# Two transformer blocks on one core: side work placed by an estimate of the engines' times instead of by fixed steps

## The chip, the cores and the metric

The kernel runs on one core of one Trainium2 chip. The metric is the device time of one execution in microseconds (us), the median of several runs; lower is better. In the rows, PE is TensorE (matmuls; PEld is its loading of weights, which overlaps them), DVE is VectorE, ACT is ScalarE, POOL is GpSimd and SP is SyncE, which here only issues weight loads.

## What is computed

One call runs two transformer blocks over 256 tokens of width 2048, all in fp32. Cut to what matters:

```python
# first block
proj = rms_norm(x) @ w_in                      # attention q, k, v; hgrn q, f, i, g; two gates
y_attn = sliding_window_attention(rotary(q), rotary(k), v, sinks)
o = hgrn2_recurrence(hq, hf, hi, lb)           # a gated linear recurrence, 8 heads of 128
y_hgrn = rms_norm(o) * silu(hg)
merged = sigmoid(gate_a) * (y_attn @ w_ab) + sigmoid(gate_b) * (y_hgrn @ w_hb)
x = x + rms_norm(merged @ w_out)
x = x + rms_norm((silu(gate) * up) @ w_down)   # feed-forward
x = x + rms_norm((p @ w_pp) * sigmoid(rms_norm(x) @ w_pg))
# second block
proj = rmsnorm(x) @ w_in_2                     # sparse attention (indexer, top 64 keys) and fox attention
x = x + concat(dsa_mixer(...), fox_mixer(...)) @ w_o
x = x + conv_ffn(rmsnorm(x))                   # conv of width 3 over tokens between w_up and w_down
return rmsnorm(x, final_g)
```

## The kernel before

All weights are read once, in pieces of 256 rows by 512 columns. SP loads a piece into a staging tile `stg`; ACT rounds it to fp32r in a `ring` tile (L283); DVE subtracts to get the rest (L289); and PE multiplies in `Core.step` (L335) with three products each of high and low parts, for one of the two tiles t of 128 tokens. One such step is six matmuls of 128x512, and order prints it as one row with x6; the pieces and the steps on PE follow a list made before anything is emitted (`Core.plan`). A cast is written AHEAD_HI = 12.0 us ahead of the step that reads it, by the list's own time, and its DVE counterpart 11.0 us ahead.

Everything else is side work: norms, the transposes of activations (L350), softmax, the recurrence, the gates, the conv. Each piece of it is a Python generator. While `Core.run` writes the weight steps, it calls `Core.pump` once for each TICK = 1.4 us of the list's time, about once a step. A generator that says `yield N` is left alone for N pumps. What it writes when it goes on enters all engines' queues there, so N sets how many steps stand on PE between a side product and its reader, and also how many casts stand ahead of the reader on ACT. Engines run their queues in order. Where a generator asks for a PSUM bank (`get("sd")`), it waits until the bank has been given back in program order. Before the change N is a constant for each place: 3 in the recurrence `hgrn` between the decays and the products that read them, SWA_LEAD = 7 and Y_SOFT = 7 in the attention `swa`, FLIP_OUT = 5 and FLIP_IN = 10 around the two DMAs of a token transpose.

Three places matter below. In `hgrn` a half-step is: two matmuls L813 and L814, ACT's Exp L817, two products of its result, on POOL L820 and on DVE L821, then `yield 3`, then the small matmuls L827 that read both products. Two such chains w = 0, 1 run side by side, with 16 half-steps each. In `swa` the transposes L610 are evacuated by ACT (L612) and read by L626 and L627; later transposes L660 to L662 are evacuated by L663 and read by L670. In `conv` (and in the first feed-forward's `gate`) a projected tile, written by ACT at L1231, is transposed by DVE (L366), written to DRAM by POOL (L370), read back by POOL (L376), and then copied and scaled by ACT (L1560, L1565).

Of the kernel before, what the change touches and what calls it, by code (L numbers as in the profile page):

```python
# [18 lines left out]
P = 128  # L19
# [7 lines left out]
SWA_LEAD = 7  # L27
# [6 lines left out]
Y_SOFT = 7  # L34
# [3 lines left out]
B_LEAD = 1  # L38
LO_LAG = 2
FLIPS = 8  # L40
FLIP_OUT = 5
FLIP_IN = 10
# [5 lines left out]
N_COLS = 171 + 3 * 88  # L48

# [34 lines left out]
class Core:  # L84
    def __init__(self, ctx, tc, aps, out):
        self.tc, self.nc, self.i, self.out = tc, tc.nc, aps, out
        nc = self.nc
        self.mq = nc.gpsimd
# [40 lines left out]
    def take(self, cls, dt=F32):  # L129
        if cls in self.free_banks:  # L130
            self.free_banks[cls] -= 1
            self.serial += 1
            return self.psum.tile([P, 512], F32, tag=cls, bufs=4, name=f"{cls}_{self.serial}")
# [11 lines left out]
    def get(self, cls, n=1, dt=F32):  # L145
        while not self.can(cls, n):
            yield 1
        r = [self.take(cls, dt) for _ in range(n)]
        return r[0] if n == 1 else r

    def put(self, cls, n=1):
# [3 lines left out]
        else:  # L155
            self.free_banks[cls] += n
            assert self.free_banks[cls] <= 4, cls
# [10 lines left out]
    def col(self, n):  # L168
# [4 lines left out]
        return r  # L173

# [21 lines left out]
    def pump_until(self, cond, what):  # L196
        for _ in range(20000):
            if cond():
                return
            self.pump()  # L200
# [178 lines left out]
    def x_block(self, src, xt, j, t, goff):  # L379
# [5 lines left out]
        while xt.blk[j] is True:  # L385
            yield 1
        bank = yield from self.get("sd")
# [127 lines left out]
    def start(self):  # L515
        nc = self.nc
        sl = [slice(512 * j, 512 * j + 512) for j in range(4)]
        for j in range(4):
# [3 lines left out]
            yield 2  # L522
        for t in range(2):
# [20 lines left out]
    def head_kv(self, c):  # L544
# [3 lines left out]
        def done(t):  # L548
# [10 lines left out]
            yield 7  # L559
# [38 lines left out]
    def swa(self, q, rot):  # L598
# [20 lines left out]
        for pr in range(4):  # L619
            j = 4 * q + pr  # L620
            qt = qts[pr // 2][:, (pr % 2) * 256 : (pr % 2) * 256 + 256]
            l0, l1 = yield from self.get("s2", 2)
# [31 lines left out]
            yield Y_SOFT  # L654
            t0, t1 = yield from self.get("s2", 2)
            b0 = yield from self.get("sd")
            b1 = yield from self.get("sd")
# [9 lines left out]
            yield 3  # L667
# [23 lines left out]
    def head_hq(self, c, g):  # L691
# [3 lines left out]
        def done(t):  # L695
# [6 lines left out]
            yield 4  # L702
# [8 lines left out]
    def head_hf(self, c, g):  # L711
# [4 lines left out]
        def done(t):  # L716
            here.append(t)
            if len(here) == 1:
                return
            G = self.grp(g)  # L720
            yield from self.wait("lb")
            lb, om = yield from self.get("s2", 2)
            for a, r in enumerate((lb, om)):
                self.mq.dma_start(r, bass.AP(tensor=self.d_lb.tensor, offset=self.d_lb.offset + 1024 * a + 512 * g,
                                             ap=[[0, P], [1, 512]]))
# [12 lines left out]
            G["lf"] = yield from self.get("s8", dt=F32R)  # L738
            hi = G["lf"][:, 0:1024].rearrange("p (t n) -> p t n", t=2)
# [5 lines left out]
            yield 7  # L745
            while "qk" not in G:
                yield 1
            for u in range(2):
                bank = yield from self.get("sd")
# [44 lines left out]
    def hgrn(self, g, w):  # L794
# [4 lines left out]
        for hh in (w, w + 2):  # L799
# [5 lines left out]
            for t in range(2):  # L805
                kt, qt = k[:, t * P : (t + 1) * P], q[:, t * P : (t + 1) * P]
                pick = sc[:, t * P : (t + 1) * P]
                for half in range(2):
                    e = yield from self.get("sd")
# [12 lines left out]
                    yield 3  # L822
# [16 lines left out]
                    if half == 1 and t == 1:  # L839
                        x = yield from self.get("sd")  # L840
# [5 lines left out]
            yield 2  # L846
# [17 lines left out]
            yield 2  # L864
# [32 lines left out]
    def branch(self, c, ab, j, first):  # L897
# [13 lines left out]
        def done(t):  # L911
# [13 lines left out]
            yield 4  # L925
# [54 lines left out]
    def boundary(self, t):  # L980
# [14 lines left out]
        yield B_LEAD  # L995
# [29 lines left out]
    def ffn_up(self, c, i):  # L1025
# [3 lines left out]
        def done(t):  # L1029
# [7 lines left out]
            yield FLIP_OUT  # L1037
# [7 lines left out]
            yield FLIP_IN  # L1045
# [29 lines left out]
    def ple_p(self):  # L1075
# [3 lines left out]
        for t in range(2):  # L1079
            raw = yield from self.get("s2")  # L1080
            self.mq.dma_start(raw[:, 0:256], self.i["p"][t * P : (t + 1) * P, :])
            yield 6
# [21 lines left out]
    def head_small(self, c):  # L1104
# [5 lines left out]
        def done(t):  # L1110
# [30 lines left out]
            yield 6  # L1141
# [11 lines left out]
            S["kz"] = yield from self.get("s2")  # L1153
            bank = yield from self.get("sd")
# [68 lines left out]
    def two(self, c, then):  # L1223
# [5 lines left out]
        def done(t):  # L1229
# [4 lines left out]
            if len(got) == 2:  # L1234
                yield 3
# [3 lines left out]
    def pair_T(self, got, a, dst):  # L1239

        bank = yield from self.get("sd")
# [7 lines left out]
    def head_iq(self, c, q):  # L1249
# [3 lines left out]
        def then(got):  # L1253
# [10 lines left out]
            for p in range(4):  # L1264
                for t in range(2):
                    n = P * (t + 1)
                    bank = yield from self.get("sd")
# [71 lines left out]
    def softmax_pv(self, qt, kt, bias, v, dst, pr, scale, need=None):  # L1339

        nc = self.nc
        l0, l1 = yield from self.get("s2", 2)
# [21 lines left out]
        yield Y_SOFT  # L1364
        t0, t1 = yield from self.get("s2", 2)
        b0 = yield from self.get("sd")
        b1 = yield from self.get("sd")
# [8 lines left out]
        yield 3  # L1376
# [671 lines left out]
```

## Time and profile before

| | |
|---|---|
| median of 3 runs | 2660.38 us (2657.01 to 2662.94) |
| the profiled execution | 2657.43 us |
| its span | 2655.6 us |
| PE busy | 2623.4 us, 99% |
| DVE, ACT, POOL busy | 1613.8, 1339.5, 361.8 us |
| L335 on PE, the weight steps | 2508.7 us busy, 10824 matmuls |

The span lies inside the execution's own time; 1.8 us lie around it. Idle time of an engine in the rows stands behind its busy time, with what ended it (the releaser). A view of waits sums that idle time by line and releaser; a timeline lists instructions in order of their starts, neighbours of one kind merged (x2 and more), with the idle time ahead in brackets; a table of stretches gives each engine's busy time in each.

### The profile page before, as it was taken

To read this page: it belongs to the slowest core of one execution; us is meant where nothing else is said; L and a number is where in the kernel's file an instruction comes from. 1 tells how busy PE (TensorE), PEld (TensorE's weight loads), DVE (VectorE), ACT (ScalarE), POOL (GpSimd) and SP (SyncE) were. 2 spreads that over 40 slices of the span, in tenths; PEclk is the share of its full clock that TensorE was granted. 3 is DMA by queue.
4 is the path that set the end of the run, shared out by engine and by line. 5 is a ranking of instruction groups with operands and counts; after the bars stand their busy time and mean duration, and the time that the engine had idled before them with its cause. 6 is when DMAs were issued, how large, how long until landed. Compare 5 with 4: busy or idle time off the path is not lost.

```text
span 2655.6 us, 32471 instructions
## 1 busy us (share of the span) xinstructions
PE 2623.4 (99%) x11929; PEld 2168.9 (82%) x11929; DVE 1613.8 (61%) x2145; ACT 1339.5 (50%) x2004; POOL 361.8 (14%) x420
## 2 busy tenths in 40 slices
PE   8999999999999999999999999999999999999998
PEld 7887788888888888888887788788888888888887
DVE  6765676465555454545457564855557757575757
ACT  6545654454553443443435574554556636464644
POOL 1341031020100000000001110100013212121211
PEclk9999999999999999999999999999999999999999
DMA  7545445666676565656566666456556766575754
GB/s 256 165 129 171 161 147 185 221 230 243 219 243 219 212 210 206 217 201 223 209 209 220 235 213 184 137 175 214 191 198 235 250 221 237 209 242 207 246 202 146
DMA packets 154431, 547.02 MB, mean 206 GB/s; under 512 B 19512, under 2 KB 22096, under 8 KB 153248
## 3 DMA queue, kind: packets, MB, share of 16 engines
q1 hardware_dynamic: 133504, 476.83, 51.9%
q0 software_dynamic: 19472, 67.54, 7.8%
q8 instruction: 93, 1.52, 0.2%
q10 hardware_dynamic: 1296, 0.59, 0.1%
q14 instruction: 66, 0.54, 0.1%
HBM read 514.46 MB, written 30.43 MB: 205 GB/s over the span
## 4 chain that ended last, share of the span: by engine, by line
PE 95%; ACT 1%; DVE 1%; POOL 1%; issue 1%; DMA 0%; SPq 0%; ACTq 0%; POOLq 0%; DVEq 0%
PE mm L335 89%; PE sd L350 1%; PE sd L827 1%; DVE ring L289 1%; ACT ring L283 0%; PE sd L1272 0%; PE sd L1349 0%; POOL s L820 0%; ACT s L394 0%; PE sd L670 0%; PE sd L1381 0%; PE sd L627 0%; PE sd L1244 0%; DMA s<-in_x_dram 0%; PE sd L813 0%
## 5 line engine op out<-in xcount | busy, mean ns | idle before, releaser
L335 PE MATMUL mm<-ring,s 128*128 128x512 f32 (+1 forms) x10824 | 2508.7, 391 | 8.0 <-ACT ring L283 6.3
L335 PEld LDWEIGHTS mm<-ring,s 128*128 128x128 f32 x10824 | 2023.4, 188 | 430.8 <-ACT ring L283 7.6
L289 DVE TENSOR_TENSOR ring<-stg,ring 128x1024 fp32r<-128x1024 f32 (+1 forms) x904 | 1088.9, 1252 | 406.2 <-ACT ring L283 399.4
L283 ACT CAST ring<-stg 128x1024 fp32r<-128x1024 f32 (+1 forms) x904 | 904.5, 1049 | 159.3 <-PE mm L335 93.8
L370 POOL DMA_DIRECT2D flip<-s x66 | 37.0, 562 | 973.0 <-DVE s L366 967.4
L1231 ACT ACTIVATE s<-mm,ss 128x512 f32<-128x512 f32 x60 | 41.5, 691 | 237.6 <-PE mm L335 224.9
L1068 DVE TENSOR_TENSOR s<-mm,s 128x512 f32<-128x512 f32 x72 | 48.7, 687 | 86.5 <-PE mm L335 86.3
L1020 ACT ACTIVATE s<-mm,ss 128x512 f32<-128x512 f32 x22 | 15.2, 690 | 139.1 <-PE mm L335 139.1
L1033 DVE SCALAR_TENSOR_TENSOR s<-mm,ss,s 128x512 f32<-128x512 f32 x22 | 16.1, 730 | 108.3 <-PE mm L335 108.3
L345 POOL TENSOR_TENSOR small<-small,mhalf 128x1 f32<-128x1 f32 (+1 forms) x27 | 17.5, 649 | 361.3 <-DVE small L344 328.7
L820 POOL TENSOR_TENSOR s<-s,s 128x512 f32<-128x512 f32 x32 | 53.3, 1672 | 93.8 <-ACT s L817 89.1
L356 ACT CAST s<-sd 64x256 fp32r<-64x256 f32 (+2 forms) x34 | 16.0, 470 | 88.6 <-PE sd L350 49.7
L376 POOL DMA_DIRECT2D s<-flip x66 | 50.5, 767 | 67.8 <-DMA flip<-s 39.8
L394 ACT ACTIVATE s<-sd,cols 128x128 fp32r<-128x128 f32 x160 | 45.8, 388 | 22.0 <-PE sd L350 19.1
L357 DVE TENSOR_TENSOR s<-s,s 128x512 fp32r<-128x512 f32 x22 | 15.2, 690 | 65.3 <-ACT s L356 65.3
L1584 POOL TENSOR_TENSOR s<-s,s 128x512 f32<-128x512 f32 x22 | 41.2, 1874 | 82.9 <-DVE s L1567 82.8
L350 PE MATMUL sd<-ident,s 128*128 128x128 f32 x252 | 40.8, 285 | 9.9 <-DMA ident<-in_c_ident_dram 4.0
L350 PEld LDWEIGHTS sd<-ident,s 128*128 128x128 f32 x252 | 32.4, 147 | 20.7 <-DMA ident<-in_c_ident_dram 4.0
L1565 ACT ACTIVATE s<-s,cols 128x256 f32<-128x256 f32 x88 | 48.2, 594 | 1.5
L357 DVE TENSOR_TENSOR s<-sd,s 64x256 fp32r<-64x256 f32 (+2 forms) x34 | 18.7, 549 | 47.4 <-ACT s L356 47.3
L1587 ACT CAST s<-s 128x512 fp32r<-128x512 f32 x22 | 13.6, 620 | 66.7 <-POOL s L1584 66.7
L366 DVE STREAM_TRANSPOSE s<-s 128x512 f32<-128x512 f32 x66 | 46.2, 706 | 1.6
(293 smaller groups left out, 1247.4 us busy)
## 6 DMA issues: line engine op xcount, KB each, us to landing
stg<-in_w_in_dram SPq DMA_DIRECT2D x232, 512.0 KB, 4.4
stg<-in_w_gu_dram SPq DMA_DIRECT2D x176, 512.0 KB, 5.5
stg<-in_w_dn_dram SPq DMA_DIRECT2D x176, 512.0 KB, 5.4
stg<-in_w_up_dram SPq DMA_DIRECT2D x176, 512.0 KB, 5.3
flip<-s POOLq DMA_DIRECT2D x66, 256.0 KB, 2.6
s<-flip POOLq DMA_DIRECT2D x66, 256.0 KB, 5.7
stg<-in_w_out_dram SPq DMA_DIRECT2D x32, 512.0 KB, 5.7
stg<-in_w_pg_dram SPq DMA_DIRECT2D x32, 512.0 KB, 5.5
```

What stands on the lines that cost most here:

```text
L283: nc.scalar.copy(w[:, 0, :, 0 : cc.n], stg[n_hi][0][:, :, 0 : cc.n])
L289: nc.vector.tensor_tensor(wl[:, :, 0 : cc.n], unstage(n_lo)[:, :, 0 : cc.n], wh[:, :, 0 : cc.n].bitcast(F32), op=ALU.subtract)
L335: nc.tensor.matmul(c.ps[t][:, 0 : c.n], xl if p == "C" else xh, wl if p == "B" else wh, start=n == 0, stop=n == 6 * c.nhp - 1)
L350: self.nc.tensor.transpose(bank[:, a * P : (a + 1) * P], s, self.ident)
L366: nc.vector.transpose(ts, src)
L376: self.mq.dma_start(tr.rearrange("p (i x) -> p i x", i=4), d.rearrange("(i r) (j x) -> (r j) i x", i=4, j=4))
L394: nc.scalar.activation(hi[:, a], b3[:, a], AF.Copy, scale=g[a])
L820: nc.gpsimd.tensor_tensor(k3, d3, kt[:, None, :].to_broadcast([P, 4, P]), op=ALU.mult)
L1068: nc.vector.tensor_tensor(y, ps[t], y, op=ALU.add)
L1231: nc.scalar.activation(r, ps[t], AF.Copy, scale=self.rs[t])
L1565: nc.scalar.activation(v, u, AF.Identity, scale=w[2], bias=self.cols[:, C_CB + k : C_CB + k + 1])
L1584: nc.gpsimd.tensor_tensor(o, o, g, op=ALU.mult)
```

## The change

The constants of the fixed waits are gone. A `Clock` keeps an estimate of the time of each engine. All instructions now go through a wrapper (`Watched`) that, while the program is being written, adds each one to its engine's estimate: it begins when its engine and its operands are free, and costs a formula of its size. A generator now says `yield 1` and then `ripe(operands)`: it waits, pump by pump, until the estimate has the operands there no later than the reading engine's (and PE's) present time plus RIPE = 0.3 us. `get("sd")` likewise waits for the estimated release of the bank. If the weight steps themselves are held up for more than PATIENCE = 2 pumps, the waits are let pass (`rush`). The loads of the recurrence's bounds (`lb`) are issued one tile earlier. What is computed and the weight steps' order are the same; since the wrapper issues every instruction, all instructions of the changed kernel carry one line number, L116, and their tiles tell them apart.

```diff
-SWA_LEAD = 7
-Y_SOFT = 7
-FLIP_OUT = 5
-FLIP_IN = 10
+RIPE = 0.3
+PATIENCE = 2
...
+    def there(self, ap, eng=None):
+        return max(t + (0.0 if e == eng else late) for t, late, e in (self.wrote.get(k, (0.0, 0.0, eng)) for k in self.blocks(ap)))
+    def now(self, eng):
+        return max(self.t[eng], self.t["PE"])
+    def note(self, eng, outs, ins, cost, late, dma=0.0):
+        begin = self.t[eng]
+        for ap in (*ins, *outs):
+            begin = max(begin, self.there(ap, eng))
...
+        end = self.t[eng] = begin + cost
...
+    def cost(self, op, out, ins, kw):
+        n = max(a.size() // max(1, a.shape[0]) for a in [out, *ins])
+        if op == "dma_start":
+            return (0.5, 1.9, out.size() * 4 / 340e3) if self.name == "SP" else (0.5, 4.3)
...
+        if self.name == "ACT":
+            return 0.15 + n / 1280 + (0.19 if "accum_out" in kw else 0.0), 0.15
+        if self.name == "DVE":
+            return 0.13 + n / 960, 0.15
+        return 0.3 + n / 450, 0.2
...
     def get(self, cls, n=1, dt=F32):
-        while not self.can(cls, n):
+        while not self.can(cls, n) or (cls == "sd" and not (self.rush or self.early) and not self.clk.free(cls, n)):
             yield 1
...
+    def ripe(self, *aps, eng="PE"):
+        while not (self.rush or self.early) and max(self.clk.there(a) for a in aps) > self.clk.now(eng) + RIPE:
+            yield 1
...
@@ swa
-        yield SWA_LEAD
+        yield 1
...
+        yield from self.ripe(rot[0], rot[1], self.kz)
...
+            yield from self.ripe(qt)
             l0, l1 = yield from self.get("s2", 2)
...
-            yield Y_SOFT
+            yield 1
+            yield from self.ripe(l0[:, 0:256], l1)
...
@@ hgrn
+                    yield from self.ripe(G["lf"], self.L[:, 0 : 9 * P])
                     e = yield from self.get("sd")
...
-                    yield 3
+                    yield 1
+                    yield from self.ripe(dk, dq, *(() if half else (qk,)))
                     s = yield from self.get("sd")
...
@@ conv
-            yield FLIP_OUT
+            yield 2
             for ts, d in ds:
+                yield from self.ripe(d, eng="POOL")
                 trs.append((yield from self.flip_in(d)))
                 self.drop(ts)
-            yield FLIP_IN
+            yield 2
+            yield from self.ripe(*trs, eng="ACT")
```

Three places show how it moves instructions. First, on PE in `hgrn`, before. The rows x6 are weight steps, sd_1155 and sd_1168 are the decays of the two chains (L813, L814), and the L827 rows read the products of them; s_120_1158 and s_123_1171 are those products' tiles.

```order
L813 MATMUL sd_1155<-s_45_488,s_56_599 128x512
L814 MATMUL sd_1155<-s_45_488,s_56_599 128x512
L350 MATMUL sd_1162<-ident,s_79_816 128x128 x2
L813 MATMUL sd_1168<-s_45_488,s_56_599 128x512
L814 MATMUL sd_1168<-s_45_488,s_56_599 128x512
L335 MATMUL mm_1015<-ring_1013,s_16_176 128x512 x6
L335 MATMUL mm_985<-ring_1036,s_21_225 128x512 x6
L335 MATMUL mm_1015<-ring_1036,s_21_225 128x512 x6
L827 MATMUL sd_1199<-s_120_1158 128x64 x3
L827 MATMUL sd_1207<-s_123_1171 128x64 x4
```

Between the last decay matmul and the first L827 stand three steps. After the change, again with two chains, sd_1097 and sd_1120; s_117_1100 and s_120_1123 hold their products:

```order
L116 MATMUL sd_1097<-s_45_488,s_56_599 128x512 x2
L116 MATMUL mm_1055<-ring_892,s_4_99 128x512 x6
L116 MATMUL mm_1032<-ring_940,s_10_139 128x512 x6
L116 MATMUL sd_1120<-s_45_488,s_56_599 128x512 x2
L116 MATMUL sd_1127<-s_117_1100 128x64 x4
L116 MATMUL sd_1127<-one,s_79_808 128x1
L116 MATMUL mm_1055<-ring_940,s_10_139 128x512 x6
L116 MATMUL sd_1146<-s_120_1123 128x64 x3
```

From sd_1097 to its readers stand two steps and the other chain's decays, and from sd_1120 to its reader on s_120_1123 one step and a few small matmuls.

Second, on PE at the start of `swa`, before: the transposes into sd_1573 (two of four are shown) are evacuated by ACT into the tile that L626 reads.

```order
L610 MATMUL sd_1573<-ident,s_120_1158 128x128
L610 MATMUL sd_1573<-ident,s_79_816 128x128
L626 MATMUL sd_1580<-s_98_984,s_79_816 128x256
L627 MATMUL sd_1581<-s_98_984,s_79_816 128x512
L335 MATMUL mm_1514<-ring_1468,s_10_139 128x512 x6
```

Nothing stands between them. After the change, the same two transposes' groups and the two matmuls (now 128x256 and 128x512 from s_105_1031):

```order
L116 MATMUL sd_1577<-ident,s_162_1502 128x128 x4
L116 MATMUL mm_1523<-ring_1486,s_10_139 128x512 x6
L116 MATMUL sd_1592<-s_105_1031,s_162_1502 128x256
L116 MATMUL sd_1593<-s_105_1031,s_162_1502 128x512
L116 MATMUL mm_1532<-ring_1486,s_10_139 128x512 x6
L116 MATMUL mm_1523<-ring_1508,s_16_176 128x512 x6
```

One weight step has come between the transposes and the matmuls that read them.

Third, on ACT in `conv`, before: the second tile of a chunk is written from PSUM (the first row, L1231), and the COPY of L1560 reads it after its way through DRAM.

```order
L1231 ACTIVATE s_1330_13839<-mm_13693,ss_77 128x512
L283 CAST ring_13859<-stg_121 128x1024
L283 CAST ring_13882<-stg_121 128x1024
L283 CAST ring_13898<-stg_126 128x1024
L283 CAST ring_13916<-stg_126 128x1024
L283 CAST ring_13932<-stg_4611 128x1024
L283 CAST ring_13948<-stg_4611 128x1024
L283 CAST ring_13964<-stg_4614 128x1024
L1231 ACTIVATE s_1330_13839<-mm_13852,ss_77 128x512
L283 CAST ring_13981<-stg_4614 128x1024
L1231 ACTIVATE s_1330_13839<-mm_13861,ss_77 128x512
L283 CAST ring_13999<-stg_121 128x1024
L1560 COPY s_1347_14008<-s_1330_13839 128x2x128 x2
```

Nine casts stand between, and the next chunk's two tiles. After the change, the same stretch of a chunk, with the two writes from PSUM (ACTIVATE from mm) and the COPY:

```order
L116 ACTIVATE s_1349_13858<-mm_13717,ss_77 128x512
L116 CAST ring_13860<-stg_4622 128x1024
L116 ACTIVATE s_1349_13858<-mm_13726,ss_77 128x512
L116 CAST ring_13884<-stg_121 128x1024
L116 CAST ring_13901<-stg_121 128x1024
L116 CAST ring_13919<-stg_126 128x1024
L116 CAST ring_13935<-stg_126 128x1024
L116 COPY s_1349_13858<-s_1349_13858 128x2x128 x2
```

Four casts now stand between the second write and the COPY.

## Rows read from the trace of the kernel before

**Rows 1.** Page: engines' busy us (share, instructions), then the largest group on PE.

```profile
PE 2623.4 (99%) x11929; PEld 2168.9 (82%) x11929; DVE 1613.8 (61%) x2145; ACT 1339.5 (50%) x2004; POOL 361.8 (14%) x420
...
L335 PE MATMUL mm<-ring,s 128*128 128x512 f32 (+1 forms) x10824 | 2508.7, 391 | 8.0 <-ACT ring L283 6.3
```

**Rows 2.** Waits of PE: waiting line, releaser: us in total, times, longest.

```profile
PE mm L335 <- ACT ring L283: 6.3, 3, 3.7
...
PE sd L350 <- ACT ring L283: 2.1, 1, 2.1
...
PE sd L827 <- POOL s L820: 1.1, 2, 0.6
...
PE sd L626 <- ACT s L612: 0.5, 2, 0.3
```

**Rows 3.** Stretches: start:end, length, busy us of five engines, TensorE's clock, DMA share.

```profile
0.00:22.00 22.00, 14.97 (x62) 11.73 (x63) 9.14 (x23) 13.29 (x37) 0.20 (x4) 1.00 0.70 249
...
340.00:450.00 110.00, 107.41 (x557) 90.76 (x556) 77.70 (x129) 50.55 (x82) 36.92 (x31) 1.00 0.48 156
...
1440.00:1475.00 35.00, 29.33 (x128) 23.31 (x128) 22.97 (x48) 19.42 (x44) 5.02 (x9) 0.95 0.58 199
...
1920.00:2655.60 735.60, 726.72 (x3210) 601.60 (x3209) 481.29 (x558) 392.30 (x557) 135.49 (x142) 1.00 0.63 218
sum 2655.60, PE 2623.36 PEld 2168.92 DVE 1613.79 ACT 1339.52 POOL 361.78; mean PE 187.38 PEld 154.92 DVE 115.27 ACT 95.68 POOL 25.84
```

**Rows 4.** Timeline at 392 us, a half-step with POOL free: start, us, instruction.

```profile
392.36 0.39 PE L814 MATMUL sd<-s,s 128*128 128x512 f32 x1
...
392.84 0.60 ACT L817 ACTIVATE s<-sd 128x512 f32<-128x512 f32 x1 [2.85 <-issue]
...
393.47 0.69 DVE L821 TENSOR_TENSOR s<-s,s 128x512 f32<-128x512 f32 x1 [0.17 <-ACT s L817]
393.52 1.81 POOL L820 TENSOR_TENSOR s<-s,s 128x512 f32<-128x512 f32 x1 [3.49 <-ACT s L817]
```

**Rows 5.** Timeline at 109 us, the half-steps of both chains together.

```profile
109.39 0.39 PE L814 MATMUL sd<-s,s 128*128 128x512 f32 x1
...
110.04 2.39 DVE L821 TENSOR_TENSOR s<-s,s 128x512 f32<-128x512 f32 x2 [0.27 <-ACT s L817]
110.09 3.51 POOL L820 TENSOR_TENSOR s<-s,s 128x512 f32<-128x512 f32 x2 [3.45 <-ACT s L817]
```

**Rows 6.** POOL's product, all 32: ns min/median/max, first and last start.

```profile
L820 POOL TENSOR_TENSOR s<-s,s x32: 1264/1745/2337, 85.6 to 435.6; 128x512 f32<-128x512 f32 x32
```

**Rows 7.** Timeline at 433 us, ACT held by a store, and the wait on PE behind it.

```profile
432.84 0.69 ACT L889 ACTIVATE s<-mm,ss 128x512 f32<-128x512 f32 x1 [4.09 <-DMA d_gate<-s]
...
435.58 0.50 PE L350 MATMUL sd<-ident,s 128*128 128x128 f32 x2 [2.11 <-ACT ring L283]
```

**Rows 8.** Timeline at 262 us, in the attention.

```profile
261.45 0.59 ACT L663 COPY s<-sd 128x512 f32<-128x512 f32 x1 [5.47 <-POOL s L578]
...
262.09 1.12 PE L670 MATMUL sd<-s,s 128*128 128x512 f32 x2 [0.93 <-ACT s L663]
```

**Rows 9.** Timeline at 1442 us, where the last part of the first block begins.

```profile
1442.33 0.63 ACT L964 ACTIVATE s<-s 128x512 f32<-128x512 f32 x1 [1.57 <-DVE s L963]
...
1444.44 1.03 ACT L283 CAST ring<-stg 128x1024 fp32r<-128x1024 f32 x1
...
1445.52 2.08 PE L335 MATMUL mm<-ring,s 128*128 128x512 f32 x4 [3.72 <-ACT ring L283]
```

**Rows 10.** Timeline from 2015 us, one conv chunk.

```profile
2015.88 0.69 ACT L1231 ACTIVATE s<-mm,ss 128x512 f32<-128x512 f32 x1
...
2020.67 1.45 DVE L366 STREAM_TRANSPOSE s<-s 128x512 f32<-128x512 f32 x2
...
2024.54 1.51 POOL L376 DMA_DIRECT2D s<-flip  x2 [1.57 <-DMA flip<-s]
...
2039.16 0.71 ACT L1560 COPY s<-s 128x256 f32<-128x256 f32 x2
```

**Rows 11.** Page: DMA issues, KB each, median us from issue to landing.

```profile
s<-flip POOLq DMA_DIRECT2D x66, 256.0 KB, 5.7
```

More of the change, by code (lines that the diff above doesn't have):

```diff
@@ L48, with __init__, blocks, give @@
 N_COLS = 171 + 3 * 88
+class Clock:
+    def __init__(self):
+        self.t = {"PE": 0.0, "ACT": 0.0, "DVE": 0.0, "POOL": 0.0, "SP": 0.0, "DMA": 0.0}
+        self.wrote, self.read = {}, {}
+        self.banks = {"sd": [0.0] * 4, "mm": [0.0] * 4}
+        self.side = False
+    @staticmethod
+    def blocks(ap):
+        name, dims = ap.tensor.name, list(ap.ap)
+        if ap.space == DRAM:
+            lo, step = ap.offset, 8192
+        else:
+            lo, step, dims = ap.offset % max(1, dims[0][0]), 64, dims[1:]
+        hi = lo + sum((n - 1) * abs(d) for d, n in dims)
+        return [(name, b) for b in range(lo // step, hi // step + 1)]
+    def there(self, ap, eng=None):
[6 more added lines that the diff above has]
+            begin = max(begin, self.there(ap, eng))
+        keys = [k for ap in outs for k in self.blocks(ap)]
+        for k in keys:
+            begin = max(begin, self.read.get(k, 0.0))
+        end = self.t[eng] = begin + cost
+        if dma:
+            end = self.t["DMA"] = max(self.t["DMA"], end) + dma
+        for ap in ins:
+            for k in self.blocks(ap):
+                self.read[k] = max(self.read.get(k, 0.0), end)
+        for k in keys:
+            self.wrote[k] = (end, late, "DMA" if late > 1.0 else eng)
+    def give(self, cls, n):
+        self.banks[cls] += [max(self.t["ACT"], self.t["DVE"])] * n
+        self.banks[cls].sort()
+    def free(self, cls, n):
+        return self.banks[cls][n - 1] <= self.t["PE"] + RIPE
+    def take(self, cls, ap):
+        t = self.banks[cls].pop(0)
+        for k in self.blocks(ap):
+            self.wrote[k] = (t, 0.0, None)
@@ L51, with __init__ @@
+class Chip:
+    def __init__(self, nc, clock):
+        self.tensor = Watched(clock, "PE", nc.tensor)
+        self.scalar = Watched(clock, "ACT", nc.scalar)
+        self.vector = Watched(clock, "DVE", nc.vector)
+        self.gpsimd = Watched(clock, "POOL", nc.gpsimd)
+        self.sync = Watched(clock, "SP", nc.sync)
 class XT:
@@ L717, in done @@
             here.append(t)
+            G = self.grp(g)
             if len(here) == 1:
-                return
[L720 to L725, printed above, removed]
+                yield from self.wait("lb")
+                G["lb"] = yield from self.get("s2", 2)
+                for a, r in enumerate(G["lb"]):
+                    self.mq.dma_start(r, bass.AP(tensor=self.d_lb.tensor, offset=self.d_lb.offset + 1024 * a + 512 * g,
+                                                 ap=[[0, P], [1, 512]]))
+                return
+            while "lb" not in G:
+                yield 1
+            lb, om = G["lb"]
             fs = yield from self.get("s2", 4)
@@ L994, in boundary @@
         r = self.rstd(tot, 1, D)
-        yield B_LEAD
+        yield 1
+        yield from self.ripe(r, *xs, eng="DVE")
         for j in range(4):
@@ L1375, in softmax_pv @@
         self.drop(l0, l1)
-        yield 3
+        yield 1
         if need is not None:
             yield from need()
+        yield from self.ripe(t0, t1[:, 0:256], *(v(z, a) for z in range(2) for a in range(2)))
         bo = yield from self.get("sd")
@@ L1493, in pair @@
                                   bass.AP(tensor=self.d_cum.tensor, offset=self.d_cum.offset + 256 * (h + a), ap=[[0, P], [1, 256]]))
-            yield 3
+            yield 1
+            yield from self.ripe(row, eng="DVE")
             cur = self.cm[:, P:256]
```

89 lines of the change are left out of this document (67 added, 22 removed).

## The prediction, made before the changed kernel ran

> **What bounds the kernel now.** I read the page's engine line first: PE is busy 2623.4 of 2655.6 us, and 2508.7 of that is the weight steps [rows 1]. Neither is changed in number or size, so the change can only move PE's idle time. The table of stretches says how much there is: 32.2 us, of which 7.0 lie in the first 22 us and 8.9 after 1920 us [rows 3]. In that last stretch the timeline shows PE without a gap until the end, where the last norm and store run behind the last step; no fixed wait stands there. That leaves 32.2 - 7.0 - 8.9 = 16.3 us to be won. The view of waits then says who is waited for [rows 2]: 6.3 us for ring casts that stood behind side work on ACT, another 2.1 put down to the same releaser, and small sums at single readers (1.1 in the recurrence, 0.5 in the attention). The reader is to see two things. The fixed waits hide nearly all of their chains already: 32 half-steps of the recurrence cost PE 1.1 us for POOL's product. And the price of shortening them is not bounded by 16.3 us, since every distance in the order that falls below its chain is new idle time on the engine that sets the end.
>
> The profiled execution took 2657.43 us, 2.95 under the median of the runs shown (2660.38); the sum below is made against 2657.43 and its span of 2655.6, with the 1.8 us around it kept. About 0.2%, 5.3 us, is what a measurement can tell from no change.
>
> **The recurrence, the largest term.** In a half-step PE issues L814, ACT takes the Exp, POOL and DVE make the products, and L827 reads them. With POOL free the chain from L814's start to the product's end is 393.52 + 1.81 - 392.36 = 2.97 us [rows 4]; I count 3.0 with the step to PE. With the other chain's half-step just ahead on POOL it is 110.09 + 3.51 - 109.39 = 4.21 us [rows 5], say 4.26. Of the 32 half-steps 11 lie at up to 3.3 us, 7 between 3.5 and 4.25, and 14 are longer, because casts or copies were in the way while nobody yet asked for the product.
>
> Against that stands what the order puts between L814's start and L827 on PE. A step is six matmuls of 227 ns by the spacing of their starts, 1.36 us; small matmuls go by their own spacing. Before, the shortest of the 32 distances is 4.3 us, 19 lie between 4.3 and 5.9 and the rest above; so even the 4.26 is covered, which fits the 1.1 us of waits [rows 2]. After, counted in the same way in the changed order, two are 2.24 us, three 2.95, seventeen between 3.3 and 3.7, four between 3.7 and 4.1, and six longer. The estimate behind it has the Exp at 0.55 us, POOL's product at 1.44 and some tenths between engines. It knows the queue on POOL, but 1.44 is below the median of 1.745 and far below the largest, 2.337 [rows 6].
>
> The shortfalls: were every chain free (3.0), 2 x 0.76 + 3 x 0.05 give 1.7 us. Were each as long as in the trace but capped at the crowded row's 4.26, the sum over the 32 is 13.8. With the cap at 5.3 us it is 26. All three hold with the other instructions where they are. A PE that waits also gives POOL and DVE time to empty their queues, so that the chain after a stall is nearer to the free row; I take 10, nearer to 13.8 than to 1.7, because both chains run together in most of the stretch. The 1.1 us of before is inside these distances. A gain beyond that 1.1 is excluded, since PE waits for nothing else there.
>
> The row of a free half-step shows DVE's product, 0.69 us, and POOL's starting together, and POOL's taking 1.81 where its shortest is 1.264 [rows 4, 6]. [...]
>
> **The stall at 433 us.** ACT's L889 waits 4.09 us for the store of the gate tile that it overwrites, and the squares, the norm and PE's transposes wait behind it, 2.1 us on PE [rows 7]. In the changed order the same write of the gate tile stands directly ahead of the same squares on ACT, and PE's distance there is 3.28 us as before. The estimate counts a tile's read by a DMA as over when the DMA is issued, so it doesn't see this wait. Term 0; if the store's wait goes, -2, if it falls worse, +1.
>
> **The attention.** A step now stands between the transposes L610 and the reader L626, and hides the copies between: -0.5, the whole of that wait [rows 2]. Between L662 and L670 one step stands where three stood. The free chain there is a copy of 0.59 us, but where ACT was held by L578's product on POOL, 5.47 us, the 4.1 us of three steps left PE 0.93 idle [rows 8]. That is so for two of the eight pairs, at 5.0 and 4.8 us by the timeline; with one step they would cost up to 3.7 and 3.5. The estimate follows that rotation on POOL, so that it will mostly not write the reader behind it: 0 to +7, taken +1, near the six pairs that are free.
>
> **The part from 1441 us.** Ring casts stand behind L964 and three squares on ACT, and PE waits 3.72 us [rows 9]. [...] The change writes the second set of transposes by the old rule and the first two steps later. The chain L963 to L1006 is data, not a fixed wait, and stays ahead of the casts. So -3 (most of the stall and its clock gone) to +2 (one more square ahead of the cast); I take -1.
>
> **The conv and the feed-forward.** From the write of a chunk's second tile, ending at 2016.6, to the landing of its flip, issued last near 2025.3 and taking 5.7 us, it is 14.4 us [rows 10, 11]. Before, nine casts stand behind the write and ahead of L1560, which ran at 2039.16, some 8 us after the landing. After, it is four casts in 12 of the 22 chunks and five in 10. A cast serves 12 matmuls, 2.72 us of PE, so four cover 10.9 us at PE's pace and five 13.6. ACT then idles 14.4 - 10.9 = 3.5 us at most if it keeps PE's pace, 10.2 if it has run through the four casts at once (1.05 us each). Casts are written 12 us ahead, which hides the first and just hides the second. The cover is gone where DVE or POOL add queueing to 10.2 us. Price 0 to 11 (half a microsecond in each of 22 chunks); I take +3, nearer to the covered end, because the last stretch has no gap today [rows 3].
>
> **Sum.** 10 - 0.5 + 0 + 1 - 1 + 3 = 12.5. All other moved waits end on chains with more than a step to spare: 0. So 2657.4 + 12.5 = **2670 us**, 0.4 to 0.5% slower than before.
>
> **The rivals.** (a) It does what it says and the idle time goes: readers come late enough everywhere, and casts no longer stand behind side work. [...] For it: 6.3 us hang on the order on ACT. Against it: the two largest waits hang on data and on a store that the estimate doesn't know. This ends on the other side; it decides if the stall from 1441 us falls below 1 us and the recurrence costs under 2.
> (b) No change: the chains in the recurrence are mostly free (+2), the conv is covered (0), the attention and the part from 1441 us cancel: 2655 to 2662. For it: the free row's 2.97 lies under all but five of the new distances. Against it: the crowded rows, and the 14 half-steps longer than those.
> (c) Much slower: the recurrence at the 5.3 us cap (+26) or the conv's upper end (+11) with the recurrence at 14: 2657.4 + 26 = 2683 to 2657.4 + 14 + 11 + 5 = 2687. For it: POOL's queue holds gate stores and rotations there too. Against it: PE's waits let the queues drain.
>
> **Chances.** My forecast (2663 to 2680) 0.52, (a) 0.14, (b) 0.15, (c) 0.19. The range takes in the forecast, (b), nearly all of (c) and the nearest part of (a): 2653 to 2690; about 0.12 of (a) and 0.05 above are left out. Within 0.2% of 2660.4 is 2655 to 2666: all of (b), 0.06 from the forecast's lower edge and 0.01 from (a), 0.22 in all. Faster is the rest of (a), 0.13; slower the rest of the forecast and (c), 0.46 + 0.19 = 0.65.
>
> **What would show it.** Right: new waits "sd <- POOL" and "sd <- DVE" of about 10 us in all at the recurrence's readers between 85 and 450 us, PE still idle about 2 us near 430, "ACT <- DMA s<-flip" grown over the last 700 us to some microseconds for each chunk, and PE idle there by 3. Wrong: waits in the recurrence of under 2 us (free chains), or PE waiting for ring casts after 1920 us by over 10 (the cover of 12 us too short). If the long wait near 1441 us is gone and the clock there is 1.00, rival (a) is at work.

## The result, and the profile after

The changed kernel takes 2734.91 us (median of 4, 2732.62 to 2736.31) against 2661.66 before: 1.0278 times, 95% interval 1.0265 to 1.0291. It is slower by 73 us, where 12 were forecast and the range ended at 2690. The profiled execution has a span of 2734.5 us, 78.9 more than before.

The page of the changed kernel (columns as in [rows 1]; all lines are L116 now, so tiles tell the groups apart):

```profile
PE 2653.4 (97%) x11929; PEld 2176.7 (80%) x11929; DVE 1601.8 (59%) x2145; ACT 1344.8 (49%) x2006; POOL 362.7 (13%) x420
...
L116 PE MATMUL mm<-ring,s 128*128 128x512 f32 (+1 forms) x10824 | 2533.8, 393 | 51.8 <-DVE ring L116 41.6
...
flip<-s POOLq DMA_DIRECT2D x66, 256.0 KB, 3.8
s<-flip POOLq DMA_DIRECT2D x66, 256.0 KB, 6.9
```

PE does the same 10824 weight matmuls, yet is busy 30 us longer, and the weight steps idle 51.8 us where it was 8.0. The waits of PE (line, releaser: total, times, longest):

```profile
PE mm L116 <- DVE ring L116: 41.6, 26, 3.8
PE mm L116 <- ACT ring L116: 8.9, 8, 2.0
PE sd L116 <- DVE s L116: 5.7, 8, 1.8
...
PE sd L116 <- POOL s L116: 3.8, 6, 1.2
```

The largest is for DVE's half of a ring tile, with DVE only 59% busy. DVE's cast needs ACT's, so ACT is the place to look. The stretches (columns as in [rows 3]; 1925 to the end is the last stretch, with the conv):

```profile
180.00:340.00 160.00, 160.00 (x718) 127.79 (x717) 101.15 (x176) 94.31 (x182) 17.47 (x17) 1.00 0.51 167
340.00:450.00 110.00, 102.91 (x512) 84.98 (x511) 72.10 (x123) 52.84 (x81) 37.13 (x31) 0.97 0.40 132
...
1440.00:1475.00 35.00, 33.18 (x159) 26.32 (x158) 26.09 (x59) 23.39 (x61) 6.12 (x13) 1.00 0.61 218
1925.00:2734.50 809.50, 754.47 (x3226) 612.61 (x3224) 473.90 (x561) 395.97 (x557) 138.20 (x142) 0.97 0.57 199
```

The last stretch had 8.9 us of idle time, its tail [rows 3]; now it is 55.0, and the granted clock is 0.97 where it was 1.00. Set against the same weight matmul of before (the weight steps come in one order in both, so that the n-th of 128x512 can be compared), the changed kernel is 11.1 us late at the 1,500th, near 450 us, 8.6 late at the 7,500th, near 1914, and 79.0 late at the last, the 10,728th. So 70.4 us were lost after 1914 us.

Of these, 46.1 are idle time, in 29 waits. The clock's share can't be taken from the mean of 0.97, because that takes in the tail, where PE idles in both kernels at a low clock (0.87 over the last 20.6 us of before); of the changed kernel:

```profile
1925.00:2713.00 788.00, 741.77 (x3171) 602.43 (x3170) 464.08 (x542) 389.03 (x542) 137.09 (x140) 0.98 0.58 202
2713.00:2734.50 21.50, 12.70 (x57) 10.18 (x55) 9.82 (x19) 6.94 (x16) 1.12 (x2) 0.85 0.27 98
```

Up to the last weight matmul the trace has 37.5 us at a granted clock of 0.50, in eight pieces. The matmuls in them start 427 ns apart in place of 227, which is 14.6 us more in all. Another 6 us or so stand at the waits themselves: the last matmul ahead of a wait takes 388 ns or more by the profile's modelled ends, where the next one would have started after 227. The last 4 us are spread and not placed.

ACT's waits in the whole run of the changed kernel, and then in the last stretch alone, of the changed kernel and of before:

```profile
ACT s L116 <- DMA s<-flip: 360.9, 63, 18.2
```

```profile
ACT s L116 <- DMA s<-flip: 198.6, 44, 10.1
ACT s L116 <- PE mm L116: 75.8, 5, 17.0
```

```profile
ACT s L1231 <- PE mm L335: 182.6, 22, 18.4
```

Before, ACT waited for PE once in each of the 22 chunks, 182.6 us: that was its spare time. It was uneven. Some 81 of the 182.6 us stand at the first chunks of five rows of chunks, where ACT would wait in any case, and the other 17 chunks have 6.0 on the mean, some of them hardly more than 1:

```profile
2014.36 0.69 ACT L1231 ACTIVATE s<-mm,ss 128x512 f32<-128x512 f32 x1 [1.24 <-PE mm L335]
...
2166.68 0.69 ACT L1231 ACTIVATE s<-mm,ss 128x512 f32<-128x512 f32 x1 [17.57 <-PE mm L335]
```

Now ACT waits for the flip in each chunk, 198.6 us, and for PE only at those five first ones. One chunk in the timeline of the changed kernel shows the rest (start, us, instruction, idle time ahead):

```profile
1985.45 0.69 ACT L116 ACTIVATE s<-mm,ss 128x512 f32<-128x512 f32 x1
...
1986.03 3.90 ACT L116 CAST ring<-stg 128x1024 fp32r<-128x1024 f32 x4
...
1993.28 0.76 POOL L116 DMA_DIRECT2D s<-flip  x1 [0.20 <-issue]
1999.32 0.41 ACT L116 COPY s<-s 128x256 f32<-128x256 f32 x1 [9.40 <-DMA s<-flip]
...
2009.58 3.25 PE L116 MATMUL mm<-ring,s 128*128 128x512 f32 x12 [1.39 <-DVE ring L116]
...
2013.69 0.68 ACT L116 ACTIVATE s<-mm,ss 128x512 f32<-128x512 f32 x1
```

The four casts behind the second write run at once, in 3.90 us. ACT then stands 9.40 us until the flip has landed, PE runs out of casts ten microseconds later, and the next chunk's second write comes 28.2 us after this one; over the 17 chunks with another directly behind it is 26.3 on the mean. A chunk is 96 matmuls of 227 ns on PE, 21.8 us.

### The profile page after: what moved, and what is told of

The parts are those of the page before. It is cut to its first block, busy times and chain, and to the rows that moved or that the text cites. A ratio compares the mean times of both kernels' runs of the same rounds, so it can differ in the third digit from the quotient of the medians.

```text
span 2734.5 us, 32470 instructions
## 1 busy us (share of the span) xinstructions
PE 2653.4 (97%) x11929; PEld 2176.7 (80%) x11929; DVE 1601.8 (59%) x2145; ACT 1344.8 (49%) x2006; POOL 362.7 (13%) x420
## 4 chain that ended last, share of the span: by engine, by line
PE 71%; DMA 8%; DVE 7%; issue 6%; ACT 5%; POOL 3%; ACTq 0%; SPq 0%; POOLq 0%; DVEq 0%
PE mm L116 67%; DMA s<-flip 5%; DVE s L116 5%; PE sd L116 5%; DMA flip<-s 3%; ACT s L116 3%; POOL s L116 2%; DVE ring L116 2%; ACT ring L116 2%; DMA s<-in_x_dram 0%; ACT L116 0%; DMA s<-in_p_dram 0%; POOL small L116 0%; POOL flip L116 0%; DMA s<-d_x 0%
## 5 line engine op out<-in xcount | busy, mean ns | idle before, releaser
L116 PE MATMUL mm<-ring,s 128*128 128x512 f32 (+1 forms) x10824 | 2533.8, 393 | 51.8 <-DVE ring L116 41.6
L116 PEld LDWEIGHTS mm<-ring,s 128*128 128x128 f32 x10824 | 2031.2, 189 | 493.4 <-DVE ring L116 52.5
L116 DVE TENSOR_TENSOR ring<-stg,ring 128x1024 fp32r<-128x1024 f32 (+1 forms) x904 | 1084.5, 1248 | 309.4 <-ACT ring L116 307.8
L116 ACT CAST ring<-stg 128x1024 fp32r<-128x1024 f32 (+1 forms) x904 | 904.0, 1048 | 150.0 <-PE mm L116 53.7
L116 ACT ACTIVATE s<-mm,ss 128x512 f32<-128x512 f32 x134 | 92.0, 686 | 327.7 <-PE mm L116 309.7
L116 POOL DMA_DIRECT2D flip<-s x66 | 37.2, 564 | 964.6 <-DVE s L116 960.2
L116 DVE TENSOR_TENSOR s<-mm,s 128x512 f32<-128x512 f32 x104 | 70.6, 688 | 161.2 <-PE mm L116 123.2
L116 POOL TENSOR_TENSOR s<-s,s 128x512 f32<-128x512 f32 (+2 forms) x75 | 127.4, 1702 | 187.8 <-ACT s L116 148.5
L116 DVE SCALAR_TENSOR_TENSOR s<-s,cols,s 128x255 f32<-128x255 f32 (+1 forms) x132 | 72.8, 572 | 118.9 <-ACT s L116 116.5
L116 ACT COPY s<-s 128x256 f32<-128x256 f32 x88 | 33.5, 404 | 208.0 <-DMA s<-flip 198.6
L116 ACT CAST s<-s 128x512 fp32r<-128x512 f32 (+1 forms) x49 | 30.9, 630 | 206.6 <-DMA s<-flip 162.4
L116 DVE TENSOR_TENSOR s<-s,s 128x512 f32<-128x512 f32 (+1 forms) x88 | 73.8, 844 | 96.3 <-ACT s L116 96.1
L116 ACT ACTIVATE s<-s 128x512 f32<-128x512 f32 x107 | 67.0, 633 | 127.6 <-DVE s L116 124.5
L116 PE MATMUL sd<-s,s 128*128 128x128 f32 (+3 forms) x376 | 89.5, 364 | 1.6 <-POOL s L116 1.4
L116 DVE SCALAR_TENSOR_TENSOR s<-mm,ss,s 128x512 f32<-128x512 f32 x22 | 16.1, 730 | 113.2 <-PE mm L116 113.2
L116 PE MATMUL sd<-ident,s 128*128 128x128 f32 x437 | 67.3, 280 | 15.5 <-DVE s L116 4.7
L116 PEld LDWEIGHTS sd<-ident,s 128*128 128x128 f32 x437 | 53.7, 143 | 31.3 <-DMA s<-in_x_dram 4.6
L116 DVE STREAM_TRANSPOSE s<-s 128x512 f32<-128x512 f32 x66 | 46.5, 707 | 50.6 <-ACT s L116 46.0
L116 PEld LDWEIGHTS sd<-s,s 128*128 128x128 f32 x376 | 61.6, 194 | 14.6 <-issue 4.3
L116 POOL TENSOR_TENSOR s<-s 128x512 f32<-128x512 f32 (+1 forms) x29 | 44.6, 1536 | 210.0 <-DVE s L116 169.9
L116 DVE SCALAR_TENSOR_TENSOR s<-s,cols 128x255 f32<-128x255 f32 (+1 forms) x44 | 20.3, 482 | 85.7 <-ACT s L116 85.0
L116 ACT ACTIVATE s<-sd 128x512 f32<-128x512 f32 (+2 forms) x68 | 33.5, 499 | 68.5 <-PE sd L116 38.7
```

The lines of the kernel that those rows point to most:

```text
L116: return f(out, *args, **kw)
```

## The experiments

**What holds the 70 us.** In the changed kernel only the two waits of `conv` were fixed again:

```diff
-            yield 2
             for ts, d in ds:
-                yield from self.ripe(d, eng="POOL")
                 trs.append((yield from self.flip_in(d)))
                 self.drop(ts)
-            yield 2
-            yield from self.ripe(*trs, eng="ACT")
+            yield 10
```

(with `yield 5` ahead of the loop).

> The changed kernel with the two waits of conv fixed again at 5 and 10 steps, all else as changed. Theory 1 (the reader of the flip stands too early on ACT, so that ACT idles and casts behind it come late): the 70 us that the last stretch lost come back, 2735 - 70 = 2665 us, and the wait of ACT for s<-flip falls by about 200 us. Rival 2 (the loss there comes from the other new waits, such as the estimated release of banks, or from transfers that are slower for another reason): less than a third comes back, 2710 us or more.

Measured: 2664.91 us, 1.0017 times before (1.0008 to 1.0027). That is 70.0 us less than the changed kernel, and PE has no wait for casts left in the last stretch. The change's other waits by themselves don't cause this loss.

**Position or estimate.** The kernel before, with no estimate anywhere, and `yield 4` and `yield 3` in place of FLIP_OUT = 5 and FLIP_IN = 10 in `conv`:

> The kernel before with the two waits of conv at 4 and 3 steps in place of 5 and 10, which puts four or five casts between a chunk's second write from PSUM and its reader on ACT, as the estimate does. No estimate anywhere. Theory 1 (position alone): 2662 + 70 = 2730 us, half the loss idle time and a third or more TensorE's lower clock behind the stalls. Rival 2 (it takes the estimate's other effects): under 2690 us.

Measured: 2748.26 us, 1.0325 times before (1.0306 to 1.0344). The position alone does it, and 88 us are more than the estimate's 70, though the casts are as many (4.7 on the mean; 4.5 in the changed kernel). Why it is 18 more was not tried; the flip's way out was slower there, 5.0 us against 3.8 (medians of the pages). Between the 7,500th and the last weight matmul this kernel idles 56 us, and its low clock costs some 16, an estimate from its mean clock of 0.97 after 1920 us and the 14.6 us that 37.5 us at 0.50 cost in the changed kernel: less than the third of the loss that was expected of the clock.

**A longer lead.** The changed kernel, with casts written earlier:

```diff
-AHEAD_HI = 12.0
-AHEAD_LO = 11.0
+AHEAD_HI = 18.0
+AHEAD_LO = 17.0
```

> The changed kernel with casts written 18 us ahead in place of 12, and their DVE counterparts 17 in place of 11. The reader in the conv still stands behind five or six casts. Theory 1b (the lead is what was too short): 6 us more of lead cover the waits, under 2680 us. Theory 1a (ACT's time for a chunk is over PE's): a longer lead is used up once in each of the five rows of conv chunks, so at most 5 x 6 = 30 us come back, 2705 us or more.

Measured: 2755.89 us, 1.0353 (1.0339 to 1.0367), 21 more than the changed kernel. PE's waits moved from the ring to the activations that the down projection reads:

```profile
PE mm L116 <- DVE s L116: 24.7, 11, 3.7
PE mm L116 <- ACT s L116: 19.1, 6, 4.9
PE mm L116 <- ACT ring L116: 7.7, 5, 3.4
```

What is short is ACT's time for a chunk, its waits included. With casts written earlier, the conv's own work is late instead, at the end of each row of chunks; so theory 1b fell.

**A later landing in the estimate.** In the changed kernel a POOL transfer counts 7.0 us to its landing:

```diff
-            return (0.5, 1.9, out.size() * 4 / 340e3) if self.name == "SP" else (0.5, 4.3)
+            return (0.5, 1.9, out.size() * 4 / 340e3) if self.name == "SP" else (0.5, 7.0)
```

> The changed kernel with one number of the estimate changed: a transfer issued by POOL lands 7.0 us after its issue in place of 4.3. In the conv the reader then stands behind six to nine casts in place of four or five. Theory 1a (a chunk holds ACT longer than PE needs for it: about 16 us of work and 9 of waiting against 96 matmuls of 227 ns, 21.8 us): 5 us less of waiting brings ACT under 21.8, and nearly all of the 70 us comes back, under 2680 us. Theory 1b (each wait of ACT uses up the 12 us by which casts are ahead, chunk by chunk): the loss shrinks in proportion, about 2700 us.

Measured: 2675.00 us, 1.0054 (1.0040 to 1.0067). In the last stretch it loses 4 us only, and ACT waits there for the flip

```profile
ACT s L116 <- DMA s<-flip: 33.3, 12, 4.0
```

where it was 198.6. But the same number sets other readers: 17.9 us are lost by the 3,000th of the weight matmuls, 7 more than in the changed kernel. It doesn't tell one or two casts from the step that the next runs found, since its readers are mixed: of the 17 with another chunk directly behind, 5 stand ahead of that chunk's two writes, 6 between them and 6 behind both.

**One cast or two later.** The kernel before with `yield 4` and `yield 5`:

> The kernel before with the conv's waits at 4 and 5 steps, which puts five or six casts between write and reader, one or two more than the estimate does and three or four fewer than before. Theory 1a (ACT's budget: PE kept it waiting 8.3 us for each of the 22 chunks before, and a wait for the flip costs only what goes beyond that): ACT waits some 5 us for each flip, that is covered, 2670 us or less. Theory 1b (each wait uses up the lead of the casts): about half of the 88 us of the run with 4 and 3 steps remain, 2700 us or more.

Measured: 2729.20 us, 1.0258 (1.0242 to 1.0274). Theory 1a missed it, 2670 or less. The bound of theory 1b, 2700 or more, holds, but its size doesn't: about half of the 88 us was to remain, and 69 did. ACT's wait for the flip did not shrink as it should; in the runs with 4 and 3, 4 and 5, 4 and 7 and 5 and 8 steps, in this order, each from its own kernel:

```profile
ACT s L1560 <- DMA s<-flip: 210.2, 40, 10.4
```

```profile
ACT s L1560 <- DMA s<-flip: 204.9, 42, 9.8
```

```profile
ACT s L1560 <- DMA s<-flip: 162.9, 42, 9.2
```

```profile
ACT s L1560 <- DMA s<-flip: 23.5, 13, 3.2
```

The last two are the runs made on this. The theory of spare time counted 8.3 us for every chunk, of which most chunks have less. The theory that takes its place is that what ACT waits and what it does stand in one loop: the second write, the casts behind it, the landing, the conv's arithmetic, the remaining casts, the next second write. A cast that is moved ahead of the reader then only fills time in which ACT stood. The chain that ended last (start, us, what ran) shows such a loop. In the kernel before it is PE's weight steps and nothing else in this stretch:

```profile
1932.69 703.16 PE mm L335 x3102
```

In the changed kernel it goes round by the transfers, the conv's work on DVE and POOL and the late cast, here from one chunk's flip to the next:

```profile
1993.28 7.06 DMA s<-flip
2006.87 1.53 DVE s L116
2008.47 2.21 POOL s L116
2012.31 1.46 DVE ring L116
2015.42 6.47 DMA flip<-s
2022.47 6.65 DMA s<-flip
```

> The kernel before with the conv's waits at 4 and 7 steps: seven casts between write and reader, and the reader still ahead of the next chunk's second write. Theory 4 (a loop on ACT: write, casts run at once at 1.05 us each, the flip's landing 14 us after the write, the conv's arithmetic, the rest of the casts, next write; it must stay under the chunk's 21.8 us on PE): each cast moved ahead of the reader takes 1.05 us from each of 22 loops. From 69 us at five or six casts that is 30 to 45 us lost, 2690 to 2705 us. Theory 5 (what counts is how late the reader stands, in steps): 4 and 7 steps are nearer to 5 and 10 than 4 and 3 are, under 2675 us.

> The kernel before with the conv's waits at 5 and 8 steps: one cast later than the run with 4 and 7, but now behind both writes of the next chunk in nearly all chunks. Theory 4: the flip's way no longer lies between one write and the next on ACT, so the loss goes at once, 2665 us or less. Theory 5: another 15 to 25 us less than the run with 4 and 7, but a rest of 10 us or more stays.

Measured: 2703.81 us, 1.0157 (1.0140 to 1.0174), and 2663.07 us, 1.0006 (0.9996 to 1.0016). From 4 and 5 steps (5.9 casts) to 4 and 7 (seven) it is 25.4 us less, 1.06 us for each of 22 chunks and cast; from 4 and 3 (4.7 casts) to 4 and 5 it was 19.1 us, 0.7 each. A cast takes ACT 1.05, so this fits only roughly, and only 17 of the 22 chunks have another directly behind; by 17 it would be 1.4 and 0.9. Then one cast later the last 41 us go at once, because the reader now stands behind both writes of the next chunk. ACT in the run with 5 and 8 steps:

```profile
2018.16 0.69 ACT L1231 ACTIVATE s<-mm,ss 128x512 f32<-128x512 f32 x1
2018.73 0.71 ACT L1560 COPY s<-s 128x256 f32<-128x256 f32 x2
...
2026.57 6.74 ACT L283 CAST ring<-stg 128x1024 fp32r<-128x1024 f32 x7
...
2038.39 0.69 ACT L1231 ACTIVATE s<-mm,ss 128x512 f32<-128x512 f32 x1 [5.08 <-PE mm L335]
...
2039.92 0.69 ACT L1231 ACTIVATE s<-mm,ss 128x512 f32<-128x512 f32 x1
```

The COPY reads the chunk before with no wait, ACT has 5.08 us to spare at the next write, and the second writes are 21.8 us apart, PE's own time for a chunk. In all 17 chunks with another directly behind the reader stands so. Theory 5 is out.

**The recurrence.** In the changed kernel only the half-step's `yield 1` and `ripe(dk, dq, ...)` became `yield 3` again:

> The changed kernel with the half-step of the recurrence back at three fixed steps, all else as changed. Theory 1 (the 11 us lost by 460 us are chains cut too short there): about 2735 - 10 = 2725 us, PE's waits for POOL and DVE at the side products fall from 9.5 to under 3 us. Rival 2 (the loss there comes from bank releases or from other readers that moved): 2731 us or more.

Measured: 2732.99 us, 1.0275 (1.0260 to 1.0291): 2 us, within what can be told. With the conv fixed as well:

> Both undone in the changed kernel: the conv and the half-steps are fixed, the estimate sets all the rest. If the two losses are apart, they add: 2735 - 70 - 10 = 2655 us, 0.2% under the kernel before. If one shifts into the other, 2665 us or more.

Measured: 2664.27 us, 1.0013 (1.0003 to 1.0022), 0.6 under the run with the conv alone. By the 1,500th weight matmul these two runs are still 6.4 and 8.9 us late. (Up to there they are the same kernel, and the four kernels in which only the conv differs from before lie between -0.5 and 3.2 there, so that some 3 us can't be told.) So either the half-step is not it, or the waiting moves. Next, the conv fixed and the whole function `hgrn` as before, and then the same with only the half-step's line given to the estimate again:

> The conv's waits fixed at 5 and 10 steps, and all waits inside the recurrence (not only the half-step) as before; the estimate sets the rest. Theory 1 (what the half-step alone did not give back stands at the recurrence's other readers, the transposes and the sums of a head): the 8 us that are left by 460 us go, 2664.9 - 8 = 2657 us. Rival 2 (they come from the generators around it, whose work moved): 2662 us or more.

> As the run with the conv and the whole recurrence fixed (2658.6 us), but the half-step's readers are placed by the estimate again. Theory 3 (the loss of the recurrence lies mostly at its other readers, since fixing the half-step alone gave 2 us or less): 2661 us or less. Theory 1 (my prediction: the half-step is the loss, and fixing it alone only moved the waiting to the other readers): 2664 us or more.

Measured: 2658.62 us, 0.9989 (0.9980 to 0.9998), and 2666.07 us, 1.0019 (1.0010 to 1.0028). PE's waits between 22 and 460 us, first with the recurrence as before, then with the half-step by the estimate:

```profile
PE sd L116 <- DVE s L116: 2.4, 1, 2.4
PE sd L116 <- ACT ring L116: 2.1, 1, 2.1
PE sd L116 <- POOL s L116: 1.4, 2, 0.8
```

```profile
PE sd L116 <- POOL s L116: 5.5, 7, 1.4
PE sd L116 <- DVE s L116: 4.8, 6, 1.5
```

The half-step alone costs 7.5 us (8.7 if each is set against the kernel before as run beside it), with seven short waits for POOL's product and six for DVE. Theory 1's bound was met and theory 3's was not. But the other readers alone cost nearly as much. With the conv fixed, and against the kernel before as run beside each, it is +4.4 us with the whole recurrence by the estimate, +3.8 with all but the half-step, +5.5 with the half-step alone and -3.2 with none: the two don't add, and either is enough. Where PE waits shows it too. In the changed kernel, between 22 and 460 us, 4.5 us of waits stand at the half-step's small matmuls (128x64) and 4.4 at the transposes of a head's result, as here; before they are 1.2 and 2.1, the 2.1 all at the stall of [rows 7].

```profile
381.88 0.30 PE L116 MATMUL sd<-ident,s 128*128 128x128 f32 x1 [1.75 <-DVE s L116]
```

With the half-step at three steps again the transposes keep 4.5, and its own readers wait 5.1 even so.

A longer POOL product in the estimate, with the conv fixed (`return 0.3 + n / 350, 0.2` in place of `n / 450`):

> The conv fixed as in the run before, the recurrence by the estimate, but a POOL instruction now counts 0.3 us and one per 350 elements, 1.76 us for the product of 512 (measured median 1.745, the change has 1.44). Theory 1 (the formula is too short): 4 to 6 us come back of those lost by 460 us, 2660 us. Rival 2 (the half-step's formula matters little, as fixing it at three steps gave 2 us or less): 2663 us or more.

Measured: 2663.32 us, 1.0006 (0.9997 to 1.0016). Against 1.0017 with the shorter formula that is 1 to 3 us, and the intervals overlap: open. The time itself lies on the rival's side, 2663 or more.

**The store of the gate tile.** To the kernel with conv and recurrence fixed:

```diff
             self.mq.dma_start(self.d_gate[ab, j, t], o)
+            yield 6
             self.drop(o)
```

> As the run with the conv and the whole recurrence fixed (2658.6 us), but a gate tile is given back six steps after its store is issued, so that ACT doesn't overwrite a tile that a transfer still reads. If the wait near 433 us comes from that store, it goes: 2.1 to 2.3 us less, 2656.4 us, and ACT's waits for d_gate fall to under 2 us. If another wait stands right behind it, 2658 us or more.

Measured: 2654.91 us, 0.9977 times before (0.9968 to 0.9986). ACT's wait for `d_gate<-s`, 8.3 us in the kernel that it was made from, is gone, and the stretch that [rows 3] shows with 107.41 of 110 us busy (107.05 in the kernel that it was made from) now reads

```profile
340.00:450.00 110.00, 109.17 (x561) 92.61 (x560) 77.79 (x123) 51.68 (x77) 37.04 (x30) 1.00 0.47 156
```

This kernel, with the estimate for all but the conv and the recurrence, beats both, by 0.2% and by 80 us. Of the 0.2% about half is the later giving back, which needs no estimate and was not tried in the kernel before.

## Why the prediction was wrong, point by point

**The sign** was right: PE's work is the same and distances cut below their chains are new idle time. **The place** was not: the recurrence was called the largest term, and the conv was. **The size was off by 61 us, nearly all of it the conv's term.** None of the rivals reaches the time either; (c), the nearest, had the conv at 11.

**The conv, +3 forecast (0 to 11), 70 measured.** Two sentences of that step failed. First, "if it keeps PE's pace": four casts do not cover 10.9 us. They run as soon as they are reached, 3.90 us, so the wait was at its upper end, 9.40 us and a little more at the second tile (10.2 had been worked out). Second, that a lead of 12 us "just hides the second". A lead covers one late start; this wait returns in every chunk, and the comparison that decides is a rate: what a chunk takes on ACT from one second write to the next, with the flip's landing inside, against 21.8 us on PE. It was 28.2 us in the chunk shown, 26.3 on the mean. The runs with 4 and 7 and with 5 and 8 steps show it from both sides. The prediction's own sign of being wrong came, "PE waiting for ring casts after 1920 us by over 10": it was 46.1. The reason that it gave beside it, the cover of 12 us too short, did not hold, for with 18 us the kernel was slower still. A row of the kernel before, which the prediction doesn't use, would have warned: ACT's waits for PE ahead of the chunks, 6.0 us on the mean away from the first ones, against an upper end of 10.2 us of new waiting in each. Casts per chunk and the reader's place against the next write should have been read from the order together.

**The clock** entered the forecast only at 1441 us. In the last stretch some 15 of the 70 us come from it, the 37.5 us that ran at a granted clock of 0.50 instead of 1.00. In the recurrence, too, it reads 0.97 over 110 us: up to 3.3 us beside the idle time.

**The recurrence, +10 (1.7 to 26)**: the changed kernel is 11.1 us late at 450 us, and the half-step by itself costs 7.5 to 8.7 by the pair of runs. The number fits, but in part by luck. PE's waits at side products there are 5.4 us for DVE and 3.8 for POOL, "about 10 us in all", as was written; yet 4.4 of the 5.4 stand at the transposes of a head's result, 0.9 of them at the stall near 433 us and 3.5 at others. The prediction has these others among "All other moved waits", at 0, for "more than a step to spare". That step failed. At the half-step's readers, the mechanism that it named, there are 4.5 us, and the clock adds to both. That the waits move when the half-step alone is mended was not foreseen.

**The stall at 433 us**, 0: it stayed on ACT (3.4 us for the store near 423) and shrank on PE, from 2.11 to 0.89; that the store is its cause, worth 2 to 4 us, is shown by the late drop.

**The attention**, -0.5 and +1: 180 to 340 us is now fully busy, where 1.5 us were idle before. The risk at L663 did not come. That this is because the estimate follows the rotation on POOL was argued, and no run tests it.

**The part from 1441 us**, -1: the long stall and its clock are gone (33.18 of 35 us busy at clock 1.00, against 29.33 at 0.95). No run shows the clock's share in the -1 or in its bound of -3 by itself; in the trace of before the granted clock is 0.50 from 1445.5 to 1448.9 us, right behind the wait, and the weight matmuls there start 427 ns apart in place of 227. But the changed kernel gains only 1.1 us between the 5,700th and the 6,000th weight matmul, as other waits came in near it. Kernels that are the same there as before differ by up to 3 us over these matmuls, so the gain is not clear of noise. Rival (a) was at work here and in the attention, for a few us.

## What to carry to other kernels

Here a reader that stood between two writes of its own engine put everything on its path, transfers too, into that engine's loop, 26.3 us on the mean against 21.8 on the engine that bounds; compare the two, and if the loop is longer, put the reader behind the next write (2663.07 us, against 2703.81 with the reader one cast earlier). A lead of so many microseconds pays for one delay, not for one in every piece (18 us in place of 12 cost 21 us here). An estimate that places work by when operands are ready needs a margin where the row of the trace is longer than its formula (the flip's 5.7 us [rows 11] against 4.3), because what came too early cost the engine that sets the end: 70 us in the conv. At the conv's reader what comes late cost nothing (1.0006 times before with 5 and 8 steps); elsewhere it can, since the longer landing in the estimate lost 7 us more before the conv.

## What the runs showed of the hardware that was not expected

In the changed kernel short waits cost more than their length: in the last stretch 46 us of idle time, in waits of up to 3.8 us, came with 24 us more in which PE was busy, some 15 of them at the lower clock of 0.50. The transfers' landing also moved with the order: the flip's way out took 3.8 us (median of all 66) in place of 2.6, and its way back 6.9 in place of 5.7 [rows 11]. In the run with 5 and 8 steps they were 2.6 and 6.6, with nothing lost, so a slower way back is not what costs. The way out was 2.4 to 2.6 us in four kernels without the conv's loss (before, conv and recurrence fixed, 5 and 8 steps, and the later landing, which loses 4 us there) and 3.8 to 5.0 in four with it (changed, the longer lead, 4 and 3 steps, 4 and 5). Whether that is a part of the cause or comes of it was not tried; 1.2 us in each of 22 chunks would be 26 of the 70 us at most.
